# Score products over 128 rows, and all matmul operands at one place in 512 bytes

## The chip, the core and the metric

The kernel runs on one core of a Trainium2 chip. Five engines work beside each other, each through its own queue in order: TensorE (PE, matmuls, with its weight loads, PEld), VectorE (DVE), ScalarE (ACT), GpSimd (POOL) and SyncE (SP, which issues the DMAs). The on-chip memory SBUF has 128 partitions; a tile of `[P, n]` takes n elements of every partition. PSUM takes the matmul results, in eight banks of 512 floats a partition.

The metric is the device time of one execution in microseconds, the median of several. Before the change it is 910.77 us (three runs, 908.93 to 912.34).

## The reference, cut to what matters

One decoder block over 512 tokens of width 1024, in float32. A conditioning vector gives six modulation vectors (adaLN). The modulated, normalised input is projected once and feeds two branches: MoBA attention (8 heads of 64) and RetNet retention (8 heads with keys of 64 and values of 128). Both are gated, merged and projected; then follow a squared-ReLU MLP (1024 to 4096 and back) and a last norm.

```python
h = modulate(rms_norm(x, ln1_w[l]), sh1, sc1)
proj = h @ w_in[l]
mq, mk, mv, rq, rk, rv, rg, ga, gr = jnp.split(proj, split_at, axis=-1)
...
s_own = jnp.einsum('bhqd,bhtd->bhqt', q_i, k_own).astype(jnp.float32) * scale      # MoBA scores
...
scores = jnp.einsum('bhnid,bhnjd->bhnij', qc, kc) * decay[None, :, None]           # retention scores
o_intra = jnp.einsum('bhnij,bhnje->bhnie', scores, vc)
...
merged = jax.nn.sigmoid(ga) * y_a + jax.nn.sigmoid(gr) * y_r
x = x + g1 * (merged @ w_out[l])
h2 = modulate(rms_norm(x, ln2_w[l]), sh2, sc2)
x = x + g2 * (jnp.square(jax.nn.relu(h2 @ w_ff1[l])) @ w_ff2[l])
```

The change touches the two score products, q times k over 64 channels of a head.

## The kernel before

**Precision.** Matmuls take operands in a rounded float32 form (`float32r`). To keep the accuracy of float32 each operand is split in a rounded part hi and a rest lo, and a product is three matmuls: hi hi, hi lo, lo hi (`mm3`, L214 to L217). ACT rounds a weight (`whi`, L179), POOL subtracts (`wlo`, L184, four pieces of 256 columns).

**Stages, in the order of time.** Up to about 70 us the first modulation and the first projections run (`product`, L343, with the sums of `ada_sum`, L267, on DVE). Then the MoBA heads run, h = 0 to 7, to about 240 us: for each tile of 128 keys a transpose of the probabilities (`moba_turn`, L572), the scores of the next head (`moba_scores`, L537) and the product with the values (`moba_values`, L582). Between these, `fill(n)` (L420) takes pieces of a queue of projections, so that PE has work while ACT and DVE do the softmax. From about 240 to 415 us the retention heads run in the same manner (`ret_scores`, L671, `ret_out`, L688), with the second modulation on DVE beside them. Then come the last projections, the merge and the first half of the output product (L955 to L977, to about 515 us), the rest of it and the norm, and from about 545 us the MLP: `ff1_part` (L1061) and the loop over `ff2_step` (L1144).

**Scores.** Two heads form a pair i; head s of the pair (s = 0, 1) has its 64 channels in partitions 64 s to 64 s + 63. The tile `qs` holds, for head s, hi of q in the head's own partitions and lo of q in the other 64. The tile `kh` holds hi of k in both halves. So the first score matmul (L547, L682) runs over 128 rows and gives hi hi + lo hi at once. The second one (L548, L683) adds hi of q times lo of k: it takes the 64 own rows of `qs` and of `kl`, in which lo of k of both heads lies, each in its own half. There are 8 heads with 4 tiles in either branch, so 64 such pairs of matmuls.

**The queue `later`.** The rotation of q and k and the splits into `qs`, `kh` and `kl` are small functions on ACT and DVE; they stand in the deque `later` and are recorded one or two at a time by `do_later` (L458), or all that are needed when a head's scores come up (`while h // 2 not in stacked`, L539, L672). `kl` has two buffers, one a pair. PE's order is as written (`manual_schedule`); DVE, ACT and POOL are ordered by the tile framework's scheduler in the two branches.

**Where tiles lie.** Pools lay their tiles one behind another in every partition, each rounded up to 32 bytes, from the left or from the right end of SBUF. In the built program before the change these are the starting bytes of matmul operands, modulo 512: weights `whi`, `wlo` 288; `hh`, `hl`, `mh`, `ml`, `fh`, `fl`, `woh`, `wol` 352; `qs`, `kh`, `kl` 288; tiles of the right side (`h2h`, `h2l`, `ah`, `zh`, `vm`, `vh`) and `th`, `tl` 480. Slices of these in a matmul start whole multiples of 512 bytes further on, so an operand keeps its place. In the MLP the moving operand and the stationary one stand at different places: 480 and 288 in `ff1_part`, 288 and 352 in `ff2_step`. In `out_product` (L1018) both stand at 352.

Of the kernel before, what the change touches and what calls it, by code (L numbers as in the profile page):

```python
# [8 lines left out]
F32 = mybir.dt.float32  # L9
F32R = mybir.dt.float32r  # L10
# [4 lines left out]
P = 128  # L15
D = 1024
S = 512
NT = S // P
# [9 lines left out]
def block_kernel(  # L28
# [27 lines left out]
    ACT, DVE, POOL, PE = nc.scalar, nc.vector, nc.gpsimd, nc.tensor  # L56
    dma = nc.sync.dma_start

    def pool(name, side="left"):
        stack = ExitStack()  # L60
        p = stack.enter_context(tc.tile_pool(name=name, bufs=1, side=side, reuse_waits="tile"))
        return stack, p
# [11 lines left out]
    def ps(tag):  # L74
        return banks["pool"].tile([P, 512], F32, name=f"ps_{tag}", tag=tag, bufs=banks["tags"][tag])
# [3 lines left out]
    g_stack, G = pool("G")  # L79
# [37 lines left out]
    for t in range(NT):  # L117
# [6 lines left out]
    start = tc.manual_schedule(  # L124
        engines={mybir.EngineType.PE, mybir.EngineType.DVE, mybir.EngineType.Activation, mybir.EngineType.Pool}
    )
# [16 lines left out]
    DVE.tensor_mul(cact, ccol, csig)  # L143

    cols = G.tile([P, 72], F32, name="cols")
    cols1 = G.tile([P, 72], F32, name="cols1")

    def param_columns():
        cols_ps = ps("O")
# [226 lines left out]
    a1_stack, A1 = pool("A1")  # L376
# [76 lines left out]
        )  # L453


    later, stacked = deque(), []

    def do_later(n):  # L458
        for _ in range(min(n, len(later))):
            later.popleft()()  # L460

    def rope(i, part, a, stack):

# [20 lines left out]
    def halves(s):  # L484
        return slice(64 * s, 64 * s + 64), slice(64 - 64 * s, 128 - 64 * s)

    def stack_q(i, t):
# [7 lines left out]
        later.extend((lambda: part(0), lambda: part(1)))  # L495
        qk[i] = [q]

    def stack_k(i, t):
        kh = A1.tile([P, 2, S], F32R, name="kh", tag="kh", bufs=2)
        kl = A1.tile([P, S], F32R, name="kl", tag="kl", bufs=2)  # L500

        def copies(s):
            own, other = halves(s)
            ACT.activation(kh[own, s, :], t[own, :], AF.Copy)
            ACT.activation(kh[other, s, :], t[own, :], AF.Copy)

        def rest(s):
            own, _ = halves(s)
            DVE.tensor_sub(kl[own, :], t[own, :], kh[own, s, :].bitcast(F32))

        later.extend((lambda: copies(0), lambda: rest(0), lambda: copies(1), lambda: rest(1)))
        later.append(lambda: stacked.append(i))
        qk[i] += [kh, kl]


    vm = []
# [10 lines left out]
    qk = [None] * 8  # L527
# [4 lines left out]
    def rotate_k(i, a):  # L532
        rope(i, 1, a, lambda t: stack_k(i, t))
# [3 lines left out]
    def moba_scores(h, t):  # L537

        while h // 2 not in stacked:  # L539
            do_later(1)  # L540
        q, kh, kl = qk[h // 2]
        s, pb = h % 2, 64 * (h % 2)
        own = slice(pb, pb + 64)
        n = (t + 1) * P
        ts = slice(t * P, n)
        sc = ps("S")
        PE.matmul(sc[:, :n], q[:, s, ts], kh[:, s, :n], start=True, stop=False)  # L547
        PE.matmul(sc[:, :n], q[own, s, ts], kl[own, :n], start=False, stop=True)  # L548
        pr = A1.tile([P, S], F32, name="pr", tag="pr", bufs=4)
        st = A1.tile([P, 8], F32, name="stat", tag="stat", bufs=6)  # L550
        DVE.tensor_tensor(sc[:, ts], sc[:, ts], cap, op=ALU.min)
        if t >= 2:

            ACT.activation(pr[:, 0:256], sc[:, 0:256], AF.Copy, scale=1.0 / 256, accum_out=st[:, 0:1])
            DVE.tensor_scalar(st[:, 1:2], st[:, 0:1], 0.0, 0.0, op0=ALU.mult, op1=ALU.is_equal)
            DVE.tensor_scalar(st[:, 2:3], st[:, 1:2], -0.5, 2e38, op0=ALU.add, op1=ALU.mult)
            DVE.tensor_scalar(st[:, 3:4], st[:, 2:3], 3.4, None, op0=ALU.mult)
            DVE.tensor_scalar(sc[:, 0:256], sc[:, 0:256], st[:, 3:4], None, op0=ALU.min)
        DVE.tensor_reduce(st[:, 4:5], sc[:, :n], axis=AX.X, op=ALU.max)
        DVE.tensor_scalar(st[:, 5:6], st[:, 4:5], -0.125, None, op0=ALU.mult)  # L560
        ACT.activation(pr[:, :n], sc[:, :n], AF.Exp, bias=st[:, 5:6], scale=0.125, accum_out=st[:, 6:7])
        DVE.reciprocal(st[:, 7:8], st[:, 6:7])
        ACT.activation(pr[:, :n], pr[:, :n], AF.Copy, scale=st[:, 7:8])
        probs[h][t] = pr

    def split_tiles(src, n, el):
        th = A1.tile([P, S], F32R, name="th", tag="th", bufs=2)
        tl = A1.tile([P, S], F32R, name="tl", tag="tl", bufs=2)
        last = split(src[:, :n], th[:, :n], tl[:, :n], ACT, el)
        return th, tl, last  # L570
# [60 lines left out]

    eh = A1.tile([P, 224], F32R, name="eh")
    es = A1.tile([P, 4], F32R, name="es")
    low = A1.tile([P, 1], F32, name="low")

# [26 lines left out]
    def decay_table(h):  # L664
        dec = A1.tile([P, S], F32, name="dec", tag="dec", bufs=2)
        dma(dec, k_decay[h])
        return dec
# [3 lines left out]
    def ret_scores(h, kt):  # L671
        while 4 + h // 2 not in stacked:  # L672
            do_later(1)
        q, kh, kl = qk[4 + h // 2]
        s, pb = h % 2, 64 * (h % 2)
        own = slice(pb, pb + 64)
        if kt == 0 and h < 7:
            decs[h + 1] = decay_table(h + 1)
        n = S - kt * P
        js = slice(kt * P, (kt + 1) * P)  # L680
        sc = ps("S")
        PE.matmul(sc[:, :n], kh[:, s, js], q[:, s, kt * P :], start=True, stop=False)  # L682
        PE.matmul(sc[:, :n], kl[own, js], q[own, s, kt * P :], start=False, stop=True)  # L683
        pr = A1.tile([P, S], F32, name="pr", tag="pr", bufs=4)
        DVE.tensor_mul(pr[:, :n], sc[:, :n], decs[h][:, :n])
        return split_tiles(pr, n, DVE)
# [51 lines left out]

    mod2 = G.tile([P, 2, 8], F32, name="mod2")

    def ada_steps(work, which, eng, dst=None):
        todo = [(i, n0, k2) for i in which for n0 in range(0, D, 256) for k2 in range(4)]
# [126 lines left out]
    for t in (3, 2, 1, 0):  # L872
        moba_scores(0, t)
        fill(2)
        do_later(2)
    fill(1)
    for h in range(8):
        if h == 2:
            one_hots()
        o = ps("O")  # L880
        for kt in range(NT):
            if kt == 0:
                fill(1)
            th, tl, _ = moba_turn(h, kt)
            for t in ((3,), (2,), (1, 0), ())[kt]:
                if h < 7:
                    moba_scores(h + 1, t)
            fill(1)
            do_later(1)
            fill(1)  # L890
            moba_last = moba_values(h, kt, o, th, tl)
            do_later(1)
# [12 lines left out]
    advance(background, moba_last)  # L905
    steps = [(h, kt) for h in range(8) for kt in range(NT)]
    ahead = ret_scores(0, 0)
    fill(2)
    squares = None
    for i, (h, kt) in enumerate(steps):  # L910
        if kt == 0:
            o = ps("O")
            ret_silu(h)
        th, tl, _ = ahead
        if i + 1 < len(steps):
            ahead = ret_scores(*steps[i + 1])
        fill(1)
        do_later(2)
        if h == 6:
            ret_norm(kt)  # L920
        squares = ret_out(h, kt, o, th, tl)
        fill((2 if kt else 3) if h < 6 else 1)
        if kt == 0 and h:
            ret_variance(h - 1, *last)
        if kt == 3:
            last = squares
        if h == 5 and kt == 2:
            ret_rstd(0)
        advance(background)
# [40 lines left out]
    for i2 in range(4):  # L970
# [3 lines left out]
        for k in (2 * i2, 2 * i2 + 1):  # L974
            for t in range(NT):
                ts = slice(t * P, (t + 1) * P)
# [289 lines left out]
```

## Time and profile before

| | us |
|---|---|
| median of 3 runs | 910.77 |
| the profiled execution | 911.24 |
| its span, first to last instruction | 909.2 |
| PE busy | 878.2 |
| POOL busy | 501.6 |
| DVE busy | 465.6 |
| ACT busy | 409.1 |
| DMA, mean rate over the span | 119 GB/s |

The span is cut in stretches by stage; what an engine does is read in each of them. A matmul's duration in the rows holds the time in which it drains, and the next one runs into it: what a stream of matmuls costs is read from the starts. A matmul's form is written rows*columns of the array, then result: `64*128 64x512` is one that uses 64 rows with a moving operand of 512 columns.

### The profile page before, as it was taken

How to read it: one execution, taken by the hardware profiler on the slowest of the kernel's cores; microseconds unless marked ns; L12 is line 12 of the kernel's file. 1: busy time of each engine (PE TensorE's matmuls, PEld its weight loads, DVE VectorE, ACT ScalarE, POOL GpSimd, SP SyncE). 2: the span in 40 equal slices, each digit the busy share in tenths (PEclk: the TensorE clock that was granted, in tenths of full speed). 3: DMA queues.
4: the chain of work that ended last, by engine and by line, in shares of the span. 5: the costliest groups of instructions: out<-in, count | busy, mean ns of one | idle time of the engine just before them, and what ended most of it. 6: DMA issues, size and time to landing. Idle time of an engine off the chain costs nothing.

```text
span 909.2 us, 11772 instructions
## 1 busy us (share of the span) xinstructions
PE 878.2 (97%) x4138; PEld 708.5 (78%) x4138; DVE 465.6 (51%) x887; ACT 409.1 (45%) x697; POOL 501.6 (55%) x606
## 2 busy tenths in 40 slices
PE   7889999999999999999999889999999999999996
PEld 4667777789777888778888679888888888888885
DVE  5885676777776868883186776003304011122225
ACT  4446888986744636645232254222222211112124
POOL 3456343625543654564755475967777754444454
PEclk9899999999999999999999999999999999999999
DMA  9955222321353343422454733533432222222202
GB/s 273 277 152 166 66 77 64 94 70 47 117 160 120 118 149 115 151 71 70 139 172 152 251 109 95 158 98 114 138 102 94 95 93 93 96 95 97 100 30 93
DMA packets 104426, 108.41 MB, mean 119 GB/s; under 512 B 4832, under 2 KB 93232, under 8 KB 104368
## 3 DMA queue, kind: packets, MB, share of 16 engines
q1 hardware_dynamic: 104224, 107.41, 38.2%
q8 instruction: 32, 0.52, 0.2%
q14 instruction: 26, 0.21, 0.1%
q10 hardware_dynamic: 144, 0.26, 0.1%
HBM read 105.55 MB, written 2.10 MB: 118 GB/s over the span
## 4 chain that ended last, share of the span: by engine, by line
PE 79%; DVE 10%; DMA 5%; ACT 2%; POOL 2%; SPq 1%; issue 1%; POOLq 0%; DVEq 0%; ACTq 0%
PE ps_acc L215 21%; PE ps_acc L216 20%; PE ps_acc L217 20%; DMA ada_raw<-in_w_ada_dram 2%; DVE adaacc L267 2%; PE ps_S L217 2%; PE ps_S L216 2%; PE ps_S L215 2%; POOL wlo L184 1%; PE ps_S L683 1%; DVE adaacc L271 1%; PE ps_S L548 1%; DMA raw<-in_w_in_dram 1%; PE ps_PT L576 1%; PE ps_PT L216 1%
## 5 line engine op out<-in xcount | busy, mean ns | idle before, releaser
L184 POOL TENSOR_TENSOR wlo<-raw,whi 128x256 fp32r<-128x256 f32 x500 | 384.5, 800 | 272.6 <-ACT whi L179 265.0
L179 ACT ACTIVATE whi<-raw 128x1024 fp32r<-128x1024 f32 x126 | 132.5, 1056 | 196.5 <-PE ps_O L217 108.8
L215 PE MATMUL ps_acc<-hh,whi 128*128 128x512 f32 x304 | 125.4, 412 | 0.4 <-ACT sw L469 0.4
L217 PE MATMUL ps_acc<-hh,wlo 128*128 128x512 f32 x304 | 119.6, 393 | 0.0
L216 PE MATMUL ps_acc<-hl,whi 128*128 128x512 f32 x304 | 118.9, 391 | 0.0
L216 PE MATMUL ps_acc<-h2l,whi 128*128 128x512 f32 (+1 forms) x288 | 106.7, 371 | 0.9 <-POOL h2l L224 0.6
L215 PE MATMUL ps_acc<-h2h,whi 128*128 128x512 f32 (+1 forms) x288 | 106.6, 370 | 0.0
L217 PE MATMUL ps_acc<-h2h,wlo 128*128 128x512 f32 (+1 forms) x288 | 106.5, 370 | 0.0
L223 DVE CAST fh<-act 128x512 fp32r<-128x512 f32 x32 | 15.6, 495 | 137.7 <-PE ps_O L216 132.9
L215 PEld LDWEIGHTS ps_acc<-hh,whi 128*128 128x128 f32 x304 | 57.1, 188 | 17.0 <-issue 4.9
L217 PEld LDWEIGHTS ps_acc<-hh,wlo 128*128 128x128 f32 x304 | 57.1, 188 | 13.1
L216 PEld LDWEIGHTS ps_acc<-hl,whi 128*128 128x128 f32 x304 | 57.2, 188 | 9.9
L216 PEld LDWEIGHTS ps_acc<-h2l,whi 128*128 128x128 f32 x288 | 54.3, 189 | 11.2 <-POOL h2l L224 0.8
L217 PEld LDWEIGHTS ps_acc<-h2h,wlo 128*128 128x128 f32 x288 | 54.1, 188 | 10.1
L215 PEld LDWEIGHTS ps_acc<-h2h,whi 128*128 128x128 f32 x288 | 54.1, 188 | 9.9
L216 PE MATMUL ps_acc<-wlo,fh 128*128 128x512 f32 (+1 forms) x136 | 52.7, 387 | 0.0
L215 PE MATMUL ps_acc<-whi,fh 128*128 128x512 f32 (+1 forms) x136 | 52.7, 387 | 0.0
L217 PE MATMUL ps_acc<-whi,fl 128*128 128x512 f32 (+1 forms) x136 | 52.6, 387 | 0.0
L782 DVE SCALAR_TENSOR_TENSOR ada_acc<-ada_raw,cact,ada_acc 128x256 f32<-128x256 f32 x48 | 34.2, 712 | 34.7 <-DMA ada_raw<-in_w_ada_dram 33.8
L1117 ACT ACTIVATE relu<-ps_acc 128x512 f32<-128x512 f32 x32 | 18.9, 589 | 67.8 <-PE ps_acc L217 64.9
L758 DVE TENSOR_TENSOR g<-g,ps_acc 128x256 f32<-128x256 f32 x8 | 3.3, 418 | 89.7 <-PE ps_acc L757 89.7
L1118 POOL TENSOR_TENSOR act<-relu 128x512 f32<-128x512 f32 x32 | 34.6, 1082 | 20.0 <-ACT relu L1117 20.0
(283 smaller groups left out, 1898.4 us busy)
## 6 DMA issues: line engine op xcount, KB each, us to landing
raw<-in_w_ff_dram SPq DMA_DIRECT2D x64, 512.0 KB, 3.3
raw<-in_w_in_dram SPq DMA_DIRECT2D x32, 512.0 KB, 3.8
ada_raw<-in_w_ada_dram SPq DMA_DIRECT2D x64, 256.0 KB, 3.1
raw<-in_w_in_dram SPq DMA_DIRECT2D x36, 256.0 KB, 3.5
wada<-in_w_ada_dram SPq DMA_DIRECT2D x32, 256.0 KB, 5.2
x<-in_x_dram SPq DMA_DIRECT2D x8, 512.0 KB, 5.5
raw<-in_w_ret_o_dram SPq DMA_DIRECT2D x8, 512.0 KB, 3.6
dec<-in_k_decay_dram SPq DMA_DIRECT2D x8, 256.0 KB, 4.5
```

Of the source, the lines that this page charges most:

```text
L179: ACT.activation(hi, raw, AF.Copy)
L184: eng.tensor_sub(lo[:, qs], raw[:, qs], hi[:, qs].bitcast(F32))
L215: PE.matmul(o, lh, rh, start=first, stop=False)
L216: PE.matmul(o, lh, rl, start=False, stop=False)
L217: PE.matmul(o, ll, rh, start=False, stop=last)
L223: eh.tensor_copy(hi, src)
L267: DVE.scalar_tensor_tensor(a[k % 2], ada[j][:, k, :], cact[:, k : k + 1], a[k % 2], op0=ALU.mult, op1=ALU.add)
L271: DVE.tensor_add(a[0], a[0], a[1])
L548: PE.matmul(sc[:, :n], q[own, s, ts], kl[own, :n], start=False, stop=True)
L782: eng.scalar_tensor_tensor(acc, raw[:, 0, :], cact[:, 2 * k2 : 2 * k2 + 1], acc, op0=ALU.mult, op1=ALU.add)
L1117: ACT.activation(r, a, AF.Relu)
L1118: POOL.tensor_mul(act[n], r, r)
```

## The change

It has two parts.

**Score product.** `kl` becomes two lasting tiles, `kls[0]` and `kls[1]`, one for each head s of a pair. POOL sets the half of the other head to zero once. DVE writes lo of k into the own half, as before. The second score matmul takes all 128 rows of `qs` and of `kls[s]`. Since there is now one tile for each s, lo of k of pair i may be written only after the scores of pair i - 1 with the same s. The entry in `later` that writes it carries the number of the head it has to wait for (`2 * i - 2 + s`), and `do_later` stops before it until that head's last score product is recorded (`scored`).

**Places.** `cols1`, `eh` and the number of `stat` buffers are made larger and `mod2` is allocated earlier, so that every tile behind them moves by 64, 128 or 192 bytes (or more in the pool `A1`). In the built program all the operands named above then start at 480 modulo 512.

```diff
-    cols1 = G.tile([P, 72], F32, name="cols1")
+    cols1 = G.tile([P, 72 + 32], F32, name="cols1")[:, :72]
+    mod2 = G.tile([P, 2, 8], F32, name="mod2")
...
-    later, stacked = deque(), []
+    later, stacked, scored = deque(), [], set()
 
     def do_later(n):
         for _ in range(min(n, len(later))):
-            later.popleft()()
+            if isinstance(later[0], tuple):
+                if later[0][0] not in scored:
+                    return
+                later.popleft()[1]()
+            else:
+                later.popleft()()
...
+    kls = [A1.tile([P, S], F32R, name=f"kl{s}") for s in range(2)]
+    for s in range(2):
+        POOL.memset(kls[s][halves(s)[1], :].bitcast(F32), 0.0)
+
     def stack_k(i, t):
         kh = A1.tile([P, 2, S], F32R, name="kh", tag="kh", bufs=2)
-        kl = A1.tile([P, S], F32R, name="kl", tag="kl", bufs=2)
...
-            DVE.tensor_sub(kl[own, :], t[own, :], kh[own, s, :].bitcast(F32))
-        later.extend((lambda: copies(0), lambda: rest(0), lambda: copies(1), lambda: rest(1)))
+            DVE.tensor_sub(kls[s][own, :], t[own, :], kh[own, s, :].bitcast(F32))
+        def rest_of(s):
+            return (2 * i - 2 + s, lambda: rest(s)) if i else lambda: rest(s)
+        later.extend((lambda: copies(0), rest_of(0), lambda: copies(1), rest_of(1)))
...
-        PE.matmul(sc[:, :n], q[own, s, ts], kl[own, :n], start=False, stop=True)
+        PE.matmul(sc[:, :n], q[:, s, ts], kls[s][:, :n], start=False, stop=True)
+        if t == 0:
+            scored.add(h)
...
-        st = A1.tile([P, 8], F32, name="stat", tag="stat", bufs=6)
+        st = A1.tile([P, 8], F32, name="stat", tag="stat", bufs=16)
...
-    eh = A1.tile([P, 224], F32R, name="eh")
+    eh = A1.tile([P, 224 + 16], F32R, name="eh")[:, :224]
...
-        PE.matmul(sc[:, :n], kl[own, js], q[own, s, kt * P :], start=False, stop=True)
+        PE.matmul(sc[:, :n], kls[s][:, js], q[:, s, kt * P :], start=False, stop=True)
+        if kt == NT - 1:
+            scored.add(8 + h)
...
-    mod2 = G.tile([P, 2, 8], F32, name="mod2")
```

PE's instructions stand in the same order as before. On DVE the second `kl` of pairs 2 to 7, and the first of pair 5, stand later. The queue of DVE before, where pair 2 is split (`attn` closes head 1; `ps_S`, `stat` and `tl` belong to the softmax of head 3 and the turn of head 2):

```order
L593 TENSOR_TENSOR attn_1165<-ps_O_1171,tmp_1364 64x512
L509 TENSOR_TENSOR kl_1267<-roped_1265,kh_1266 64x512
L223 CAST ah0_1367<-attn_1165 128x512
L551 TENSOR_TENSOR ps_S_1399<-ps_S_1399,cap_100 128x128
L509 TENSOR_TENSOR kl_1267<-roped_1265,kh_1266 64x512
L224 TENSOR_TENSOR tl_1396<-ps_PT_1390,th_1395 128x512
L555 TENSOR_SCALAR stat_1403<-stat_1403 128x1
```

Both halves of `kl` are written within four instructions. The same queue now, 22 instructions further on, where the last scores of head 3 are treated:

```order
L569 TENSOR_TENSOR ps_S_1500<-ps_S_1500,cap_100 128x128
L227 TENSOR_TENSOR tl_1497<-ps_PT_1493,th_1496 128x256
L577 TENSOR_REDUCE stat_1504<-ps_S_1500 128x1
L569 TENSOR_TENSOR ps_S_1511<-ps_S_1511,cap_100 128x128
L578 TENSOR_SCALAR stat_1504<-stat_1504 128x1
L523 TENSOR_TENSOR kl1_691<-roped_1267,kh_1268 64x512
L577 TENSOR_REDUCE stat_1515<-ps_S_1511 128x1
```

The first half (`kl0`) has kept its place behind `attn`; the second has moved behind the last score product of head 3, which reads the same tile. On POOL two settings to zero are new, where the first weights of the branch are split (`wlo`); now:

```order
L305 TENSOR_TENSOR wlo<-raw,whi 128x768
L187 TENSOR_TENSOR wlo<-raw,whi 128x256 x4
L511 MEMSET kl_690 64x512
L511 MEMSET kl_691 64x512
L187 TENSOR_TENSOR wlo<-raw,whi 128x256 x16
L658 MEMSET e_1375 128x512
```

Before, the 20 pieces of `wlo` stood in one row, with nothing between them.

## Rows read from the trace of the kernel before

**Rows 1.** The page: busy time, share of the span, instructions of each engine.

```profile
PE 878.2 (97%) x4138; PEld 708.5 (78%) x4138; DVE 465.6 (51%) x887; ACT 409.1 (45%) x697; POOL 501.6 (55%) x606
```

**Rows 2.** PE's waits, whole span: who waited for whom, us in total, times, longest.

```profile
PE ps_O L277 <- DVE adaacc L271: 8.9, 7, 2.2
...
PE ps_S L217 <- DVE ml L962: 1.7, 1, 1.7
```

**Rows 3.** Busy time by stretch: us, engines' busy us (instructions), PE clock, DMA share, GB/s.

```profile
94.00:143.00 49.00, 49.00 (x221) 38.25 (x220) 32.49 (x95) 43.03 (x93) 19.56 (x25) 1.00 0.22 65
143.00:240.00 97.00, 95.85 (x535) 79.17 (x533) 68.19 (x189) 77.73 (x166) 48.65 (x59) 1.00 0.24 71
240.00:415.00 175.00, 174.88 (x866) 140.75 (x866) 130.90 (x225) 92.02 (x150) 86.94 (x101) 1.00 0.41 127
437.00:505.00 68.00, 67.21 (x292) 53.74 (x290) 42.05 (x60) 19.29 (x28) 42.24 (x48) 1.00 0.45 147
545.00:905.00 360.00, 357.01 (x1634) 291.54 (x1632) 88.56 (x145) 96.33 (x133) 222.00 (x283) 1.00 0.31 100
```

**Rows 4.** Timeline of PE, a retention score: start us, us, operation, form, count.

```profile
250.70 0.39 PE L217 MATMUL ps_acc<-hh,wlo 128*128 128x512 f32 x1
250.92 0.28 PE L682 MATMUL ps_S<-qs,kh 128*128 128x256 f32 x1
251.13 0.38 PE L683 MATMUL ps_S<-qs,kl 64*128 64x256 f32 x1
251.44 0.50 PE L215 MATMUL ps_acc<-hh,whi 128*128 128x512 f32 x1
251.78 0.39 PE L216 MATMUL ps_acc<-hl,whi 128*128 128x512 f32 x1
252.01 0.39 PE L217 MATMUL ps_acc<-hh,wlo 128*128 128x512 f32 x1
```

**Rows 5.** Timeline of PE, a MoBA score.

```profile
104.83 0.49 PE L548 MATMUL ps_S<-kl,qs 64*128 64x512 f32 x1
105.26 0.50 PE L215 MATMUL ps_acc<-hh,whi 128*128 128x512 f32 x1
105.60 0.39 PE L216 MATMUL ps_acc<-hl,whi 128*128 128x512 f32 x1
```

**Rows 6.** Timeline of PE, the output product, both operands at 352.

```profile
514.72 0.39 PE L216 MATMUL ps_acc<-wol,mh 128*128 128x512 f32 x1
...
526.96 0.39 PE L216 MATMUL ps_acc<-wol,mh 128*128 128x512 f32 x1
```

**Rows 7.** Timeline of PE, the MLP, operands at different places.

```profile
565.07 0.39 PE L215 MATMUL ps_acc<-h2h,whi 128*128 128x512 f32 x1
...
620.84 0.39 PE L217 MATMUL ps_acc<-h2h,wlo 128*128 128x512 f32 x1
...
689.18 0.39 PE L215 MATMUL ps_acc<-h2h,whi 128*128 128x512 f32 x1
...
898.80 0.39 PE L217 MATMUL ps_acc<-whi,fl 128*128 128x512 f32 x1
```

**Rows 8.** Timeline of PE, projections behind the retention, operands at 352 and 288.

```profile
421.52 0.39 PE L215 MATMUL ps_acc<-hh,whi 128*128 128x512 f32 x1
...
433.66 0.40 PE L217 MATMUL ps_acc<-hh,wlo 128*128 128x512 f32 x1
```

**Rows 9.** Timeline of POOL, behind the first stage.

```profile
72.36 5.63 POOL L184 TENSOR_TENSOR wlo<-raw,whi 128x256 fp32r<-128x256 f32 x8 [4.00 <-ACT whi L179]
...
89.10 0.52 POOL L640 MEMSET e<- 128x512 f32 x1
```

**Rows 10.** Timeline of DVE: the second `kl` of pair 2 now stands ahead of this.

```profile
151.09 0.29 DVE L559 TENSOR_REDUCE stat<-ps_S 128x1 f32<-128x128 f32 x1
```

**Rows 11.** Timeline of PE: the first score product of head 5, which reads that half.

```profile
175.66 0.50 PE L548 MATMUL ps_S<-kl,qs 64*128 64x512 f32 x1
```

**Rows 12.** ACT's longest wait from 94 to 240 us: total, times, longest.

```profile
ACT pr L561 <- DVE stat L560: 6.2, 5, 2.1
```

More of the change, by code (lines that the diff above doesn't have):

```diff
@@ L508, in rest @@
             own, _ = halves(s)
-            DVE.tensor_sub(kl[own, :], t[own, :], kh[own, s, :].bitcast(F32))
-        later.extend((lambda: copies(0), lambda: rest(0), lambda: copies(1), lambda: rest(1)))
+            DVE.tensor_sub(kls[s][own, :], t[own, :], kh[own, s, :].bitcast(F32))
+        def rest_of(s):
+            return (2 * i - 2 + s, lambda: rest(s)) if i else lambda: rest(s)
+        later.extend((lambda: copies(0), rest_of(0), lambda: copies(1), rest_of(1)))
         later.append(lambda: stacked.append(i))
-        qk[i] += [kh, kl]
+        qk[i] += [kh]
     vm = []
@@ L540, in moba_scores @@
             do_later(1)
-        q, kh, kl = qk[h // 2]
-        s, pb = h % 2, 64 * (h % 2)
-        own = slice(pb, pb + 64)
+        q, kh = qk[h // 2]
+        s = h % 2
         n = (t + 1) * P
@@ L673, in ret_scores @@
             do_later(1)
-        q, kh, kl = qk[4 + h // 2]
-        s, pb = h % 2, 64 * (h % 2)
-        own = slice(pb, pb + 64)
+        q, kh = qk[4 + h // 2]
+        s = h % 2
         if kt == 0 and h < 7:
```

## The prediction, made before the run

> **What bounds the kernel now.** I read the page's busy line first. PE is busy 878.2 of the 909.2 us, and the nearest other engine 501.6 [rows 1]: a gain must come from PE's own time or from its waits. PE's waits come second. The longest, 8.9 us, lies in the first stage, where DVE's sums for the modulation set the pace; the change leaves those sums alone, so I count no gain before 94 us. One more matters: 1.7 us for `ml` in the merge [rows 2]. Third, the stretches. From 94 to 143 us and from 240 to 415 us PE is busy 49.00 of 49 and 174.88 of 175 us, at full granted clock (2.4 GHz, as in all rows here). ACT is busy 43.03 of 49 us in the first of them, and 92.02 of 175 in the second [rows 3]. So PE bounds both branches, and ACT follows closely in the first half of MoBA. Last I read PE's timeline, from start to start, since both parts of the change act on the distance between matmuls.
>
> **The score product.** In the retention sample, streams at 512 columns start 0.23 us apart (251.78 to 252.01). From the first score matmul (250.92, 256 columns) to the 64-row one it is 0.21 us; 256 columns at half of 0.23 would be 0.115, so 0.095 is lost on entering. From the 64-row one to the next it is 0.31 us, 0.195 too much. The matmul behind it, again over 128 rows, holds the next one off by 0.34 instead of 0.23 us, 0.11 too much [rows 4]. Together 0.40 us for each score. MoBA shows the same on the way out at 512 columns: 0.43 us behind the 64-row matmul, 0.20 more than 0.23, and again 0.34 behind the next [rows 5]. All three losses sit where the number of rows changes from 128 to 64 and back; the neighbours with 128 rows on both sides have none. After the change no such place is left in the scores. The new product has as many columns as before, and the row count does not lengthen a stream: 128-row ones run at 0.23.
>
> The old trace has no 128-row product with lo of k. Its saving is bounded by 0 (the loss stays for another reason) and 0.40 us (all of it goes). I take 0.40, since the rows next to it are of just the form that it gets. Of the 64 scores, two lie before 94 us, where PE waits for the first rotation anyhow. Of the other 62, 32 lie in the retention: 32 x 0.40 = 12.8 us. There DVE is busy 130.90 of 175 us and ACT less; with 12.8 us fewer DVE stands at 81%, so I let all of it pass.
>
> 30 lie in MoBA: 12.0 us at most. Here ACT is the next limit. In 94 to 143 us some 11 scores would take 4.4 us off, to 44.6, against ACT's 43.03 busy; ACT also waits for DVE, 6.2 us in 146 for the maximum alone, some 2 us of them here [rows 3, 12]. So that stretch will hardly go below 45 to 46 us, and about 1.5 us are given back as PE waits. From 143 to 240 us ACT has 77.73 of 97, and room. Each turn (transposes, ACT, DVE, value product) also holds one score that PE now does 0.4 us sooner, and where ACT's answer came only just in time PE will wait: another 1.5 us. Bounds of the give-back: 0 and all 12. I take 3, so MoBA gives 9.0.
>
> What is added: two settings to zero on POOL, of 64x512. One of 128x512 took 0.52 us. They stand behind the first four `wlo` pieces, and POOL then idles 4.00 us for ACT before the next eight [rows 9]: 1.0 us under that cover, price 0; without the cover 1.0 us, on the weights of the first fill. The later `kl` writes: the second of pair 2 now stands just ahead of the instruction of 151.09 us and is first read at 175.66 [rows 10, 11]: 24 us of slack for a write of under a microsecond, so price 0. It waits for no score either, since it stands behind DVE instructions that read that very score. The instructions behind it on DVE (maxima, `tl`) come later by one `kl`, which was earlier in the same queue before. Ten more `stat` buffers can only remove waits, of which I count none.
>
> **The places.** The trace has a natural experiment. In the output product both operands start at 352 modulo 512: from 514.72 to 526.96 us there are 54 distances, 12.24 / 54 = 226.7 ns each [rows 6]. In the MLP they differ: 239 distances in 565.07 to 620.84 and 899 in 689.18 to 898.80, (55.77 + 209.62) / 1138 = 233.2 ns [rows 7]. Both are the same hi and lo pattern without waits, at the same clock. So 6.5 ns a matmul, and between the two MLP stretches lie three more blocks of 95: 1423 x 6.5 = 9.3 us, all on PE, which nothing holds up there (POOL is busy 222 of 360 us, ACT and DVE under 100) [rows 3]. Projections against `hh`, at 352 and 288, start 12.14 / 53 = 229.1 ns apart [rows 8]: 2.4 ns are to be had, 1% of the 343 us from 94 to 437, 3.5 us if all of it were one stream. It is cut by scores every few microseconds, so I take 1.5 (bounds 0 and 3.5). In the merge, 437 to 505 us, the 292 matmuls would save 292 x 6.5 = 1.9 us, but PE already waits there for `ml`, from DVE [rows 2, 3]. That wait grows by as much: 0. The output product gains nothing, it is already so.
>
> Place 480 in both operands occurs in no long stream of the old trace; I take it to act as 352 does, since only the distance between the two is alike. Bounds of the MLP's part: 9.3 lost, if 480 were as much worse, and 9.3 gained; I take the gain, by the nearest row.
>
> The Trainium skill speaks against this part. "SBUF — State Buffer", section "Who interferes with whom", gives PE two independent read ports, one for the moving operand and one for weight loads, and says that PE and ACT never wait on anyone. By it the places would change nothing, and the sum would hold the scores alone. The 226.7 against 233.2 ns do not agree with it, though they come from two stages; the case is a rival below.
>
> **The sum.** 12.8 + 9.0 + 9.3 + 1.5 = 32.6 us. The profiled execution took 911.24 us, 0.5 more than the median of the runs shown; 911.2 - 32.6 = 878.6, or 878.2 from the median. I say 879.
>
> **The rivals.**
>
> *The places do nothing, or harm* (other causes give the 6.5 ns, such as what else runs in the output product's 12 us). For it: one sample, at another place. Against: 54 distances that hardly vary. The time: 911.2 - 21.8 = 889.
>
> *ACT and DVE take over in MoBA.* For it: 88% ACT from 94 to 143 us. Against: 80% later. Then MoBA gives nothing: 911.2 - 23.6 = 888.
>
> *The loss isn't due to rows.* It could belong to the end of a score's accumulation or to its fresh PSUM bank. For it: each 64-row matmul is also the last of its score. Against: other products end and begin everywhere without it. The Trainium skill, "TensorEngine Tiling (Array Packing)", section "Key Properties", has TensorE drained by a change of tiling mode, which lowers this rival's chance. Then only the places gain: 911.2 - 10.8 = 900.
>
> *Slower: one `kl` for each head side holds the queue.* The write of pair i now waits for pair i - 1, and `do_later` stops there, with the next rotations behind it. If a write came after the score that needs it, PE would stop there, up to 14 times (pairs 1 to 7). It decides from the point where a write is late by more than its slack, 24 us in the sample [rows 10, 11]; to end at 916 it would have to cost 37 us, 2.7 for each of the 14 writes beyond the slack. Nothing in the order of DVE comes near.
>
> *Both parts do nothing.* 911.
>
> **Chances.** Forecast (870 to 885) 0.66; places nothing 0.12; ACT and DVE take over 0.11; loss not due to rows 0.05; both nothing 0.03; slower 0.03. The range 869 to 892 holds the forecast and the first two rivals, 0.89 less some tails; its low end is the sum without give-back, with all of the 3.5 us and the merge's 1.9, 39.5 us off (872), and a little more. No change means within 0.5%, 4.6 us, about what a measurement of this kernel can tell. Faster 0.94, same 0.03, slower 0.03.
>
> **What would show it.** In the new profile the second score matmul has the form 128*128, and the distances around it are 0.23, 0.17, 0.12 or 0.06 us by columns, without 0.34 behind. In the MLP a thousand distances average 226 to 228 ns. PE's waits list new ones in MoBA for `th`, `tl` or `stat` of 2 to 4 us, and a longer one for `ml`. From 240 to 415 us the stretch is 13 to 14 us shorter. I am wrong if the distances in the MLP stay at 233, if the 0.31 behind a score stays, or if PE's waits in MoBA pass 8 us.

## The result, and the profile after

The changed kernel takes 889.46 us (median of four runs, 889.06 to 891.12) against 911.14 us of the kernel before, run on the same chip. The ratio is 0.977, with a 95% interval of 0.975 to 0.979: 21.7 us were gained. The forecast was 879, so the direction and the range (869 to 892) held, but a third of the expected 32.6 us is missing, and the time lies outside the 870 to 885 us that the forecast itself was given.

The busy line of the page, which answers to [rows 1]:

```profile
PE 851.1 (96%) x4138; PEld 708.8 (80%) x4138; DVE 468.0 (53%) x887; ACT 408.7 (46%) x697; POOL 506.1 (57%) x608
```

PE's busy time fell by 27.1 us, the span only by 22.2 (909.2 to 887.0): the rest of what PE saved is idle time now. PE's timeline of the retention score of [rows 4], which now starts at 245.33:

```profile
245.10 0.39 PE L220 MATMUL ps_acc<-hh,wlo 128*128 128x512 f32 x1
245.33 0.28 PE L699 MATMUL ps_S<-qs,kh 128*128 128x256 f32 x1
245.44 0.28 PE L700 MATMUL ps_S<-qs,kl 128*128 128x256 f32 x1
245.56 0.40 PE L218 MATMUL ps_acc<-hh,whi 128*128 128x512 f32 x1
245.79 0.40 PE L219 MATMUL ps_acc<-hl,whi 128*128 128x512 f32 x1
```

The starts are 0.23, 0.11, 0.12 and 0.23 us apart. Before, the same steps were 0.22, 0.21, 0.31 and 0.34. In the MLP, the four rows that answer to [rows 7] (239 and 899 distances):

```profile
552.10 0.40 PE L218 MATMUL ps_acc<-h2h,whi 128*128 128x512 f32 x1
...
606.30 0.40 PE L220 MATMUL ps_acc<-h2h,wlo 128*128 128x512 f32 x1
...
672.86 0.40 PE L218 MATMUL ps_acc<-h2h,whi 128*128 128x512 f32 x1
...
876.65 0.39 PE L220 MATMUL ps_acc<-whi,fl 128*128 128x512 f32 x1
```

(54.20 + 203.79) / 1138 = 226.7 ns, where it was 233.2. Both mechanisms are there: 0.39 us less at this score, and 6.5 ns less for each matmul of the MLP. Most of what is missing shows in PE's waits from 90 to 403 us (two branches; who waited for whom, us in total, times, longest):

```profile
PE ps_O L602 <- ACT th L224: 2.1, 4, 0.7
PE ps_O L603 <- DVE tl L227: 1.4, 4, 0.4
PE ps_PT L730 <- DVE zf L753: 1.2, 1, 1.2
PE ps_O L711 <- DVE tl L227: 1.2, 2, 0.9
PE ps_O L710 <- ACT th L224: 0.7, 1, 0.7
PE ps_O L603 <- DVE stat L573: 0.2, 1, 0.2
PE ps_O L710 <- DVE gate L717: 0.2, 1, 0.2
```

7.0 us in all. The same stretch of the kernel before has two waits:

```profile
PE ps_O L584 <- ACT th L221: 0.7, 1, 0.7
PE ps_O L585 <- DVE stat L555: 0.3, 1, 0.3
```

The stretches of both branches and of the MLP, cut at the same instructions as in [rows 3]:

```profile
92.00:138.50 46.50, 45.70 (x221) 37.48 (x220) 30.61 (x94) 41.75 (x90) 19.05 (x25) 1.00 0.23 68
138.50:234.60 96.10, 92.92 (x536) 78.65 (x535) 69.22 (x189) 79.15 (x169) 49.67 (x60) 1.00 0.23 72
234.60:402.80 168.20, 164.77 (x865) 140.43 (x864) 133.72 (x225) 91.61 (x150) 89.21 (x101) 1.00 0.43 132
531.70:883.00 351.30, 348.21 (x1633) 292.20 (x1631) 89.01 (x146) 96.04 (x133) 221.55 (x283) 1.00 0.32 102
```

From 92 to 138.5 us ACT is busy for 41.75 of 46.5 us (90%; 88% before). PE no longer fills the branches: 0.8 us short in the first of these stretches, 3.2 in the second, 3.4 in the retention.

PE's 4138 matmuls stand in the same order in both kernels, so their starts can be subtracted one by one. Summed by stretch and by kind of distance, worked out from the two traces (after minus before, us):

| before's time | all | at a change of rows | waits (over 0.23 us) | 256 columns | 512 columns |
|---|---|---|---|---|---|
| 0 to 94 | -2.1 | -0.6 | -1.4 | 0 | +0.6 |
| 94 to 240, MoBA | -3.7 | -11.0 | +5.5 | +0.9 | +0.5 |
| 240 to 415, retention | -6.7 | -11.7 | +4.2 | +1.1 | -0.3 |
| 415 to 505, with the merge | -1.1 | 0 | +0.9 | 0 | -2.0 |
| 505 to 565 | +0.5 | 0 | -0.9 | +0.5 | +0.9 |
| 565 to 902, MLP | -9.1 | 0 | 0 | +0.1 | -9.2 |
| sum | -22.1 | -23.3 | +8.2 | +2.6 | -9.5 |

(256 and 512 columns stand for matmuls of these widths away from such places; other widths make up the rest.) From 0 to 94 us this is one execution against one; the point is taken up below. The waits are larger here than in the list above, which counts PE's idle time alone: at 116.53 us, shown below, PE is idle for 0.70 us, but that start comes 1.09 us behind the one before it (115.44), where 0.23 us is usual.

### The profile page after: what moved, and what is told of

It is laid out like the page before. It is cut to its first block, busy times and chain, and to the rows that moved or that the text cites. A ratio compares the mean times of both kernels' runs of the same rounds, so it can differ in the third digit from the quotient of the medians.

```text
span 887.0 us, 11777 instructions
## 1 busy us (share of the span) xinstructions
PE 851.1 (96%) x4138; PEld 708.8 (80%) x4138; DVE 468.0 (53%) x887; ACT 408.7 (46%) x697; POOL 506.1 (57%) x608
## 4 chain that ended last, share of the span: by engine, by line
PE 63%; DVE 18%; ACT 8%; DMA 6%; issue 3%; POOL 1%; SPq 1%; ACTq 0%; DVEq 0%; POOLq 0%
PE ps_acc L218 16%; PE ps_acc L219 16%; PE ps_acc L220 16%; DMA ada_raw<-in_w_ada_dram 4%; DVE adaacc L270 3%; PE ps_S L220 2%; PE ps_S L219 2%; PE ps_S L218 2%; ACT sw L478 1%; DVE ada_acc L802 1%; DVE adaacc L274 1%; DMA wada<-in_w_ada_dram 1%; ACT whi L182 1%; DVE ada_acc L799 1%; DVE qs L502 1%
## 5 line engine op out<-in xcount | busy, mean ns | idle before, releaser
L218 PE MATMUL ps_acc<-hh,whi 128*128 128x512 f32 x304 | 121.5, 400 | 0.0
L220 PE MATMUL ps_acc<-hh,wlo 128*128 128x512 f32 x304 | 119.5, 393 | 0.0
L219 PE MATMUL ps_acc<-hl,whi 128*128 128x512 f32 x304 | 119.4, 393 | 0.0
L218 PEld LDWEIGHTS ps_acc<-hh,whi 128*128 128x128 f32 x304 | 57.6, 189 | 10.1
```

Of the source, the lines that this page charges most:

```text
L218: PE.matmul(o, lh, rh, start=first, stop=False)
L219: PE.matmul(o, lh, rl, start=False, stop=False)
L220: PE.matmul(o, ll, rh, start=False, stop=last)
```

## The experiments

**The score product alone, and the places alone.**

The first is the changed kernel without the edits below, the second the kernel before with them:

```diff
-    cols1 = G.tile([P, 72], F32, name="cols1")
+    cols1 = G.tile([P, 72 + 32], F32, name="cols1")[:, :72]
+    mod2 = G.tile([P, 2, 8], F32, name="mod2")
...
-        st = A1.tile([P, 8], F32, name="stat", tag="stat", bufs=6)
+        st = A1.tile([P, 8], F32, name="stat", tag="stat", bufs=16)
...
-    eh = A1.tile([P, 224], F32R, name="eh")
+    eh = A1.tile([P, 224 + 16], F32R, name="eh")[:, :224]
```

> The new score product with the old places (operands at 288, 352 and 480). Theory: the change of rows cost PE some 0.37 us a score, and the waits that PE got in its place in both branches belong to this part alone. Then 23.3 us go and about 9 to 10 us come back as waits: 911.1 - 23.3 + 9.5 = 897 to 898 us, distances in the MLP stay at 233 ns. Rival: the new waits come with the places or the extra stat buffers; then nothing comes back here and the time is 888 us.

> The old score product on 64 rows, all operands at 480. Theory: 1423 distances in the MLP fall from 233.2 to 226.7 ns (9.2 us), the 256-column products get slower by 4 ns each (2 us) and the projections faster by about 1 us: 911.1 - 8 = 903 us, with no new waits of PE in the branches and the 0.31 us behind a score as before. Rival 1: the places do nothing by themselves, 911. Rival 2: the parts do not add up, because places and waits hide each other; then this is below 900 or above 906.

Measured: 899.87 us (ratio 0.9885, 0.987 to 0.990) and 901.40 us (0.9903, 0.9888 to 0.9917), against 909.96. The scores gain 10.1 us and the places 8.6. Their sum, 18.7 (about 2 us either way by the two intervals), and the 20.9 to 21.7 of both together agree within what these measurements can tell. By stretch, with the same subtraction: scores_only saves 22.6 us from 94 to 415 us at the changes of rows, and that stretch is 11.1 us shorter, so half of the saving comes back there; its MLP is unchanged (0.0). In places_only the MLP is 9.1 us shorter, both branches together are 0.1 us longer, and the score stands as it was:

```profile
249.85 0.28 PE L685 MATMUL ps_S<-qs,kh 128*128 128x256 f32 x1
250.05 0.38 PE L686 MATMUL ps_S<-qs,kl 64*128 64x256 f32 x1
250.37 0.50 PE L218 MATMUL ps_acc<-hh,whi 128*128 128x512 f32 x1
250.70 0.40 PE L219 MATMUL ps_acc<-hl,whi 128*128 128x512 f32 x1
```

The 0.32 and 0.33 us behind the score belong to the old product, whatever the places. Both first rivals fall, and so does the second one of the places (below 900 or above 906). For the scores a gain of 13.8 us had been expected (897 to 898), and 10.1 came. In the trace 11.5 us came back in the branches instead of 9.5, and 2.3 us were lost in the stretch from 505 to 565 us, where TensorE's granted clock was at 1.2 GHz for two times 3.4 us, and never in that of before. That clock doesn't explain the median, though: the other three executions, at mean granted clocks of 0.992 to 0.996 against 0.988 here, took 898.7 to 900.0 us too.

**Late writes with the old product.** The changed kernel, its second score product back on the head's own 64 rows:

```diff
-        PE.matmul(sc[:, :n], q[:, s, ts], kls[s][:, :n], start=False, stop=True)
+        own, _ = halves(s)
+        PE.matmul(sc[:, :n], q[own, s, ts], kls[s][own, :n], start=False, stop=True)
```

(and the same in `ret_scores`.)

> The changed kernel with its places, its two lasting tiles for lo of k and their later writes, but with the second score product on the head's own 64 rows, as before the change. Theory: the new waits of PE come from the faster scores, not from the later writes of lo of k: then the waits for th and tl go back to the 0.7 us that they had, the 0.31 us behind each score returns, and the time is that of places_only, 901 to 902 us. Rival: the order of the writes on DVE makes the waits: then some 8 us of them stay, and the time is 908 to 910 us.

Measured: 901.94 us, ratio 0.9923 (0.9907 to 0.994), the time of places_only. The only waits of PE on `th`, `tl` or lo of k:

```profile
PE ps_O L603 <- ACT th L224: 0.7, 1, 0.7
PE ps_S L565 <- DVE kl L523: 0.3, 1, 0.3
PE ps_O L713 <- DVE tl L227: 0.2, 1, 0.2
```

So the later writes of lo of k cost nothing beside the old product, and the new waits are there only where the scores are fast. In the changed kernel, too, no wait of PE from 90 to 403 us is for lo of k. Fast scores with the early writes were not run, so that the late writes add to the other waits there is unlikely, but not excluded.

**Distances in the MLP.** In `mlp_distance_sweep` the rows of `h2h` and `h2l` lie 64 bytes further on for each k, and `fh`, `fl` begin 64 (k mod 8) bytes into a larger tile; `mlp_fine_sweep` does the same with 16 bytes. Its tiles for `fh` and `fl` are 2176 bytes long, so every second buffer stands another 128 bytes further on, and its `h2h` and `h2l` stand 128 bytes apart; the distances below are those of the built program.

```diff
-    h2h = H2.tile([P, NK, S], F32R, name="h2h")
+    h2h = H2.tile([P, NK, S + 16], F32R, name="h2h")[:, :, :S]
-        fh = F2.tile([P, S], F32R, name="fh", tag="fh", bufs=6)
+        at = slice(16 * (k % 8), 16 * (k % 8) + S)
+        fh = F2.tile([P, S + 128], F32R, name="fh", tag="fh", bufs=6)[:, at]
```

> The changed kernel, but in the MLP the operand from h2 (moving) and the operand from the squared ReLU (stationary) begin at another place for each k: the distance between moving and stationary operand runs through 0, 64, ... 448 bytes modulo 512, in the first product by the place of the moving one, in the second by that of the stationary one. Theory: what counts is the distance, not the place: at 0 a 512-column matmul takes 226.7 ns, at 64 about 229, at 192 and 448 about 233, alike in both products; at 256 columns distance 0 is the slow one, 120 ns against 115 to 117. The time is then about 889.5 + 1423 x 7/8 x 5 ns = 895 to 896 us. Rival 1: the place itself counts (352 or 480 good, 288 bad): then the two products differ at the same distance. Rival 2: the stage counts, not the place: all distances stay at 227 and the time at 889.

> The changed kernel, with the place in the MLP moved by 16 bytes for each k: distances moving minus stationary of 0, 16, ... 112 bytes in the first product and 0, -16, ... -112 in the second. In mlp_distance_sweep 0 and 256 were the best (second product 227.3 and 228.5 ns) and 64 and -64 already 230 and 233. Theory: distance 0 is an optimum, and the distances rise by some nanoseconds within 32 to 64 bytes on both sides: time 895 us. Rival: the optimum lies between, at a shift of 16 to 48 bytes, below 226 ns; then a kernel could still gain there.

Measured: 897.41 and 896.08 us, one run each. In the second product each k is a block of 24 matmuls in which only that distance differs. First and last row of four such blocks of the first sweep, at distances (moving minus stationary) 256, 192, 64 and 0:

```profile
733.03 0.39 PE L218 MATMUL ps_acc<-whi,fh 128*128 128x512 f32 x1
...
738.25 0.39 PE L220 MATMUL ps_O<-whi,fl 128*128 128x512 f32 x1
738.48 0.40 PE L218 MATMUL ps_acc<-whi,fh 128*128 128x512 f32 x1
...
743.85 0.39 PE L220 MATMUL ps_O<-whi,fl 128*128 128x512 f32 x1
...
749.65 0.39 PE L218 MATMUL ps_acc<-whi,fh 128*128 128x512 f32 x1
...
754.93 0.40 PE L220 MATMUL ps_O<-whi,fl 128*128 128x512 f32 x1
755.16 0.39 PE L218 MATMUL ps_acc<-whi,fh 128*128 128x512 f32 x1
...
760.39 0.39 PE L220 MATMUL ps_O<-whi,fl 128*128 128x512 f32 x1
```

Over 23 distances these are 227.0, 233.5, 229.6 and 227.4 ns. All blocks of both sweeps, by distance modulo 256, ns a matmul (blocks of the same distance agree within 0.4 ns, but for distance 0 with 226.7 to 227.8):

| 0 | 16 | 48 | 64 | 80 | 112 | 128 | 160 | 192 | 224 |
|---|---|---|---|---|---|---|---|---|---|
| 227.3 | 228.7 | 233.3 | 229.3 | 229.8 | 226.7 | 232.3 | 234.3 | 233.4 | 233.1 |

At 256 and 448 bytes the times are those of 0 and 192, so what repeats is 256 bytes, not 512. Only the place of the stationary operand changes here. That its distance to the moving one decides, and neither stage nor place alone, is seen at equal distances of other places: 352 and 352 in the output product [rows 6] take 226.7 ns like 480 and 480 in the MLP, and a distance of 448 takes 233.3 ns at 288 and 352 (blocks of the second product in the kernel before) and 233.4 at 480 and 32 (this sweep). Distance 0 is at the optimum (112 equals it): in this product the rival that looked for less than 226 ns falls. In the first one a few groups of 28 matmuls went below it (224.3 ns on `h2l` at a distance of 432, 225.3 on `wlo` at 272 and 225.9 on `h2h` at 256), each between neighbours that took longer. My theory was only partly right, though. The time doesn't rise steadily from 0, and the two products differ at the same distance, which the first rival had named as its sign: in the first product, where the moving operand is what is shifted, the function is another one: 64 takes 233.1 ns, and 0 and 256 are best, at 230, with the matmul on `h2l` at 235 to 236 against 226.6 in the changed kernel. What else sets it when successive moving operands differ is open. For 256 columns the sweeps show 113 to 122 ns with no order by distance.

The Trainium skill ("SBUF — State Buffer", section "Who interferes with whom") gives PE two independent read ports, one for the moving operand and one for weight loads. These blocks do not bear out an independence of that kind: nothing but the place of one operand against the other changes, and the time of a matmul goes from 227 to 234 ns with it.

**`hh` back at a distance of 64.** `hh` and `hl` 64 bytes further on, with a second pad behind them so that nothing else moves:

```diff
+    H.tile([P, 16], F32, name="pad0")
     hh = [H.tile([P, S], F32R, name=f"hh{j}", tag=f"hh{j}") for j in range(NK)]
     hl = [H.tile([P, S], F32R, name=f"hl{j}", tag=f"hl{j}") for j in range(NK)]
+    H.tile([P, 112], F32, name="pad1")
```

> The changed kernel with hh and hl (and the second half of w_out, which takes their place) 64 bytes further on, at 32 modulo 512, so that they stand to the weights as in the kernel before: 64 bytes behind. Theory: distance counts for them too: the 512-column projections go from 227.6 back to 229 to 230 ns, the value projections of 256 columns, with hh stationary, from 119.6 back to 115.4 ns; the two cancel, and the stretch from 90 to 424 us changes by less than 1 us. Rival: the 256-column products depend on the place 480 itself; then they stay at 119.6 and the stretch is 1 to 2 us longer.

Measured: 889.5 us, one run. In the value projections 256 columns take 115.7 ns (178 and 169 distances; 119.3 to 119.5 in the changed kernel, 115.2 before). The projections of 512 columns behind the retention take 230.1 ns (227.1 and 229.4). From 90 to 424 us it is 0.2 us longer. As expected: with `hh` stationary and 256 columns, distance 0 is the worse one, and it takes back what it gives the projections.

**Less work for ACT in MoBA.** Four versions take work from ACT. The scaling of the probabilities moves to GpSimd, first all of it, then that of tiles 2 and 3 alone; to the latter the second copy of hi of k is added, first of all pairs, then of pairs 1 to 3 (so the new lines stand under `if t >= 2` and `if 1 <= i < 4`, with the old ones in the other cases):

```diff
-        ACT.activation(pr[:, :n], pr[:, :n], AF.Copy, scale=st[:, 7:8])
+        POOL.tensor_scalar(pr[:, :n], pr[:, :n], st[:, 7:8], None, op0=ALU.mult)
...
-            ACT.activation(kh[other, s, :], t[own, :], AF.Copy)
+            POOL.tensor_copy(kh[other, s, :], t[own, :])
```

> The changed kernel, with the scaling of the probabilities by 1/sum (32 instructions, 17.6 us of ACT in MoBA) done by GpSimd. Theory: ACT, busy 43.5 of 48.5 us in the first half of MoBA, is what PE waits for there; with 6 us less work on ACT in that half PE's new waits of 5.5 us between 90 and 235 us shrink to 2 and the time to 886 us. Rival: PE waits for the length of the chain PSUM to th to tl within a turn, not for ACT's load; then the waits stay at 5 us or grow, since GpSimd takes longer for each, and the time is 889 to 891 us.

> As the last of the runs before, but GpSimd scales only the probabilities of tiles 2 and 3 (384 and 512 columns), which are scored first and have the longest time until their turn; ACT keeps tiles 0 and 1. In the trace of that run the waits of PE for th fell by 4 us, and one new wait of 2.1 us stood before a transpose, since the small scaling of tile 0 was behind four weight pieces on GpSimd. Theory: PE's waits in MoBA come from ACT's load; without that one wait they go from 5.5 us to about 1.5, and the time from 889.5 to 885 to 886 us. Rival: the gain in the trace was the new wait's own slack, which ACT and DVE used to catch up; then the waits for th come back and the time stays at 888 to 890 us.

> As large_scales_on_gpsimd, and the second copy of hi of k (16 of 0.63 us on ACT, one for each head of both branches) is made by GpSimd too. Theory: in the retention PE waits 0.9 and 0.3 us at 363 us for a th that stands behind two of these copies on ACT; that goes, the other waits there (for tl and zf, DVE's) stay: 884 to 885 us. Rival: the copy on GpSimd comes late behind weight pieces and a first score of a pair waits for it; then the time is 886 us or more and PE's waits name kh from GpSimd.

> large_scales_on_gpsimd, with the second copy of hi of k on GpSimd for pairs 1 to 3 alone (MoBA without its first pair). In kh_copy_on_gpsimd the stretch from 90 to 235 us was 2.0 us shorter than in large_scales_on_gpsimd, but PE waited 2.5 us more for the first pair's copy at 82 us, with 0.9 us at a lower clock behind it, and 1.0 us more in the retention. Theory: these two losses came with those pairs alone; without them the time is 884 us. Rival: the 2.0 us were luck of the order, and the time stays at 886.

Why ACT's load makes the wait is seen at its longest place in MoBA. PE, then ACT, of the changed kernel (PE transposes a tile to `ps_PT`, ACT makes `th` of it, PE multiplies it with the values):

```profile
112.80 0.28 PE L594 MATMUL ps_PT<-ident,pr 128*128 128x128 f32 x1
...
115.44 0.39 PE L220 MATMUL ps_acc<-hh,wlo 128*128 128x512 f32 x1
116.53 0.33 PE L602 MATMUL ps_O<-th,vm 128*128 128x128 f32 x1 [0.70 <-ACT th L224]
```

```profile
112.50 1.06 ACT L182 ACTIVATE whi<-raw 128x1024 fp32r<-128x1024 f32 x1
...
114.95 1.01 ACT L581 ACTIVATE pr<-pr,stat 128x384 f32<-128x384 f32 x2
115.85 0.37 ACT L579 ACTIVATE pr<-ps_S,stat 128x128 f32<-128x128 f32 x1
116.10 0.21 ACT L579 ACTIVATION_READ_ACCUMULATOR pr<-ps_S,stat 128x1 f32 x1
116.19 0.28 ACT L224 ACTIVATE th<-ps_PT 128x128 fp32r<-128x128 f32 x1
```

The transpose was done by 113.1, but ACT was never idle and came to `th` at 116.19. With all scalings on GpSimd (889.64 us, ratio 0.9767, 0.9742 to 0.9792) this wait is gone. The stretch from 138 to 234 us is 2.6 us shorter, but the one ahead of it 1.4 us longer, since a small scaling now comes late, behind four weight pieces:

```profile
118.19 2.80 POOL L187 TENSOR_TENSOR wlo<-raw,whi 128x256 fp32r<-128x256 f32 x4
120.97 0.59 POOL L581 TENSOR_SCALAR pr<-pr,stat 128x128 f32<-128x128 f32 x1
```

PE waits 2.0 us for it. So the verdict on the time alone (no gain) would have been the rival's; the rows gave the theory its next version. With the large scalings alone: 886.24 us (0.973, 0.9711 to 0.975), 2.9 us off MoBA, about as expected. With every second copy of hi of k as well: 886.89 us (0.9748, 0.9728 to 0.9767), no gain. MoBA lost another 2.0 us, but the first pair's copy stands behind six weight pieces, where PE waits for it for 4.0 us instead of 1.5, and the retention is 1.0 us longer than with the large scalings alone: its wait for `th` is gone, but those for `zf` and `tl`, both DVE's, are 3.4 us instead of 2.3. Without these pairs: 884.03 us, ratio 0.9709 (0.9696 to 0.9723), 5.75 us below the changed kernel as it was measured again beside it (889.78, the experiment that follows). What stays of PE's waits for `th`, `tl` and `stat` in MoBA:

```profile
PE ps_O L608 <- ACT th L224: 1.3, 3, 0.7
...
PE ps_O L609 <- DVE tl L227: 0.6, 2, 0.4
PE ps_O L609 <- DVE stat L576: 0.4, 1, 0.4
```

ACT, busy for 90% of the first stretch in the changed kernel, is busy for 37.91 of 44.9 us (84%) there. This is the fastest version of the study.

**The changed kernel again.**

> The changed kernel once more, for its own profile beside the next one. Theory: the 2.3 us that the first trace of it gained before 70 us and the two stretches of 3.4 us at the half clock (86 and 492 us) differ from one execution to the next and are no part of the change; the waits in MoBA (5.5 us) and in the retention (4.2 us) and the 226.7 ns of the MLP stand at the same places again. Time 889 to 890 us. Rival: the clock falls at the same two places again, behind the same waits, and so belongs to the change.

Measured: 889.78 us, ratio 0.9772 (0.9753 to 0.9792). The waits stand where they stood (`th` 2.4, `tl` 1.4, `zf` 1.1, `tl` 0.9 us), and the MLP agrees within 0.01 us. TensorE's clock shows 1.2 GHz at 494 us again (in the first trace from 491.9 to 495.3), but not at 86 us, where the first trace has these rows:

```profile
86.88 0.63 PE L220 MATMUL ps_acc<-hh,wlo 128*128 128x512 f32 x1
87.31 0.63 PE L218 MATMUL ps_acc<-hh,whi 128*128 128x512 f32 x1
87.73 0.63 PE L219 MATMUL ps_acc<-hl,whi 128*128 128x512 f32 x1
```

The start to start is 0.43 us there, which makes 1.6 us over the 3.4. But changed_again, without it, has PE wait 1.0 us for `sw` of ACT at 91.7 us, and the first trace does not; behind that the two are only 0.3 us apart. In hh_moved_by_64, and in mlp_fine_sweep, which is the changed kernel up to the MLP, it is the other way round: half clock at 86 us and none near 494. So neither place belongs to the change for certain; each lies at or just behind a wait of PE. What the one near 494 us costs, these traces don't tell: from 437 to 520 us (by the time of before) changed_again gains 1.0 us with it, hh_moved_by_64 gains 1.5 and mlp_fine_sweep nothing without it.

## Why the prediction was right in direction and 10.5 us off in size

The forecast was 870 to 885 us, at a chance of 0.66, and missed. The range up to 892 held because it was made wide enough for two rivals, and by the time alone each of these, at 889 and 888 us, would have done better than my sum. What was right is seen in the parts.

**The loss at a change of rows (0.40 us a score, 24.8 us for 62): right.** 22.7 us went from 94 to 415 us, 0.37 a score. The rival that blamed something other than rows is out: scores_only has the gain without the places, and late_kl_with_64_rows loses it again with everything else kept.

**The places in the MLP (1423 x 6.5 = 9.3 us): right, 9.2.** The bound for place 480 was needless caution: the distance decides. The rival "places do nothing" is out (places_only).

**What comes back as waits: the step that failed.** I let all of the retention's 12.8 us pass, "since DVE stands at 81%", and took 3 us for MoBA. By starts, 5.5 us came back in MoBA and 4.2 in the retention, and late starts below 0.23 us add to that: scores_only gave back 11.5 us of 22.6. The listed waits for `th`, `tl` and `stat` in MoBA, 3.7 us, did fall within the 2 to 4 us that I had named (1.0 of them stood there before), but they are only the idle time. But a mean busy share was the wrong test for the retention. PE waits at single places where several pieces of work stand in a queue: `th` at 363.8 us behind three copies into `kh`, for pair 7,

```profile
361.89 0.63 ACT L518 ACTIVATE kh<-roped 64x512 fp32r<-64x512 f32 x1 [2.97 <-DVE roped L490]
362.55 0.63 ACT L519 ACTIVATE kh<-roped 64x512 fp32r<-64x512 f32 x1
363.19 0.63 ACT L518 ACTIVATE kh<-roped 64x512 fp32r<-64x512 f32 x1
363.84 0.42 ACT L224 ACTIVATE th<-pr 128x256 fp32r<-128x256 f32 x1
```

with ACT busy for only 54% of the branch. The rival "ACT and DVE take over in MoBA" was half right: of the 11 us MoBA gained only 3.7. ACT's load was the cause of the larger part, as the GpSimd versions show: with the last of them MoBA gains 8.3. For the retention the traces name the waits; taking them away was not tried beyond the `kh` copies, where DVE's waits grew as ACT's went. What bounds it is open.

**The projections against `hh` (1.5 us): failed, about 0.** I measured 512 columns alone. In places_only they gain 1.4 us from 94 to 437 us, but the 256-column products of the same stretch lose 1.6, and the first part of the MLP's first product another 0.4. The 384 value products against `hh` had their duration in the old trace; I did not read it.

**The merge (0): wrong by a little.** Its streams gained 1.7 us, and the waits there grew by 0.9, not by all of it.

**The prices at nothing** (POOL's settings to zero, the later `kl` writes) held. The rival "slower, one `kl` holds the queue" is out: the late writes with the old product take the time of places_only.

**Not in the sum:** the stretch before 70 us is 2.3 us shorter in the trace. Those of scores_only and places_only, too, are 2.2 and 1.9 us shorter there than the one trace of before. Since the parts gain less by medians (10.1 and 8.6) than by traces (11.2 and 11.0), this is likelier that one trace than the change. The other traces say the same: all twelve are shorter there than that of before, by 0.4 to 2.3 us, and changed_again, the same kernel, by 1.3.

Of the 10.5 us, then, 6.7 are waits beyond the 3 counted, 3.9 the columns at `hh` and in the first MLP part, and 1.5 the size of the loss per score. The merge and the first 70 us give 3.1 back, and small rests, the clock at 86 us among them, make up the 1.5 left.

## What to carry to other kernels

When one engine bounds a stage and gets faster, don't ask whether the others have room on average. Go through its waits-to-be one by one, and see how long before its use each operand was ready: the smallest slack is where the gain stops. Measure a place or layout effect for each width that shares the operand. And when a move to an idle engine shows no gain, read the waits before dropping it: here one late instruction took back 1.6 of the 2.9 us that MoBA had gained without it.

## What the runs showed of the hardware that was not expected

- A 512-column matmul in a dense stream (the MLP's second product) takes 226.7 to 234.3 ns by the relative place of its moving and stationary operands, with a period of 256 bytes, not 512; of the distances tried 0 and 112 bytes are best, 160 is worst. In the first product the function is another one.
- The 256-column value products go the other way: 119.4 ns at distance 0 and 115.2 to 115.7 where the moving operand starts 64 bytes below the stationary one, modulo 512.
- TensorE's granted clock fell to 1.2 GHz for 3.4 us at or behind waits of PE near 86 and 494 us, in some traces and not in others where PE's instructions up to there are the same.
